# Sums of squares and means added up on VectorE and finished by one matmul, and the compressed scores of both key-value groups in one pass

## The chip, the cores and the metric

The kernel runs on one core of a Trainium2 chip. The metric is the device time of one execution in microseconds (us). TensorE (PE) does the matmuls, VectorE (DVE) and ScalarE (ACT) the elementwise work, GpSimd (POOL) a few fills, SyncE (SP) issues the transfers. Sums over partitions, which no elementwise engine does along the rows of a tile, are made by a matmul with a matrix of equal numbers as weights.

## The reference, cut to what matters

Two layers of a decoder trunk on 256 tokens of 2048 channels. The parts that the change touches are these sums:

```python
def rms_norm(x, g, eps=EPS):
    y = x32 * lax.rsqrt(jnp.mean(x32 * x32, axis=-1, keepdims=True) + eps)
...
    # conformer_conv, 512 channels
    mu = jnp.mean(h32, axis=-1, keepdims=True)
    var = jnp.mean(jnp.square(h32 - mu), axis=-1, keepdims=True)
...
    # nsa_attention: 8 query heads, 2 key-value groups, 15 compressed blocks
    s = jnp.einsum('bgrtd,bgnd->bgrtn', q, kc) * scale
    p_cmp = masked_softmax(s, cmp_mask)
    o_cmp = jnp.einsum('bgrtn,bgnd->bgrtd', p_cmp.astype(vc.dtype), vc)
...
    # hybrid_mixer: four groups of 512, each with its own norm, then one projection
    y = rms_norm(y, group_norm.reshape(N_GROUPS, GROUP_WIDTH)).reshape(B, T, MIX_WIDTH)
    return y @ w_o
...
    # each layer
    x = x + g1 * hybrid_mixer(h, ...)
    h = rms_norm(x, norm_ffn[l]) * (1.0 + sc2) + sh2
    x = x + g2 * conv_glu_ffn(h, ...)
```

## The kernel before, in words

The residual x lies transposed in SBUF: 16 chunks of 128 channels by 256 tokens. Each large product runs over weight blocks of 128 rows by 1024 columns. `load_w` (L204 to L220) has SP load a block (`raw`, four buffers), ACT round it to the fast matmul format (`hi`, L217, three buffers), and DVE take the rest (`lo` = raw − hi, L219, three buffers). `gemm_t` (L233) then does, for each of the K chunks, 24 matmuls of 256 columns on TensorE: for each of 8 output chunks hi·x, hi·xl and lo·x, x and xl being the same two parts of the activation. So every chunk needs one cast of ACT and one `lo` of DVE.

DVE also computes the modulation vectors (`ada_dot`, L159): 384 products of a 128 by 1024 block of weights with the conditioning vector, each block loaded by SP into one of three buffers `adaw`. `tick` puts them between the weight loads as filler of low priority, and the framework's scheduler settles the order of each engine's instructions when the kernel is built; the engines run their lists in that order. So a changed number of instructions in front of a place can change the order there.

A layer goes: mixing (projections, latent attention, convolution, sparse attention `nsa_group`, stick-breaking attention `sb_attn`), the output projection `wo`, the feed-forward part (11 up groups, two down projections). Four places sum over channels and are changed:

- `Stats` (L311 to L333): the sum of squares of x for the next RMSNorm, over the 16 chunks. It is called while the output chunks of the `wo` product come out (both layers), and of the last down projection of layer 0: three instances. For every two chunks ACT squares (`sq`, L320); in the first 8 chunks DVE adds the two (L324) and one fp32 matmul with ones accumulates into `ss`; in the last 8 chunks two matmuls do. `finish` takes Ln and Exp on ACT. Then `norm_chunk` makes the 16 chunks h of the feed-forward input: DVE `t` (L338), ACT `act` (L342), DVE the rest of `act` (L343), with 12 buffers `act`, so that 12 chunks are made at first.
- `group_norm_t` (L439): the norm of one group's 512 channels, used for the convolution's output and for the stick-breaking output y3, whose result is the last input of `wo`. Four fp32 matmuls (L445).
- `conv_ln` (L570): mean `mu` (L573) and variance `va` (L579) of the convolution's 512 channels, four fp32 matmuls each.
- `heads(g)` (L877): the compressed branch of group g: 8 matmuls `sc` (L890) of 15 columns, a softmax of small DVE operations, two transposes `tpx`, the product `poc`; then the two long branches of the same group.

## Time and profile before

| | us |
|---|---|
| median of 3 runs (lowest, highest) | 2482.93 (2482.63, 2484.76) |
| the profiled execution | 2479.15 |
| its span | 2476.8 |
| PE busy | 2413.6 |
| DVE busy | 1853.5 |
| ACT busy | 1165.0 |

The times within the trace count from the span's start. Outside the span lie 2479.15 − 2476.8 = 2.35 us. An fp32 matmul stands in the trace as two rows of half the work each, so "x8" of such a matmul are 4 instructions of the program; of the fast format, one row is one instruction.

### The profile page before, as it was taken

To read this page: it belongs to the slowest core of one execution; us is meant where nothing else is said; L and a number is where in the kernel's file an instruction comes from. 1 tells how busy PE (TensorE), PEld (TensorE's weight loads), DVE (VectorE), ACT (ScalarE), POOL (GpSimd) and SP (SyncE) were. 2 spreads that over 40 slices of the span, in tenths; PEclk is the share of its full clock that TensorE was granted. 3 is DMA by queue.
4 is the path that set the end of the run, shared out by engine and by line. 5 is a ranking of instruction groups with operands and counts; after the bars stand their busy time and mean duration, and the time that the engine had idled before them with its cause. 6 is when DMAs were issued, how large, how long until landed. Compare 5 with 4: busy or idle time off the path is not lost.

```text
span 2476.8 us, 46041 instructions
## 1 busy us (share of the span) xinstructions
PE 2413.6 (97%) x18720; PEld 2330.1 (94%) x18720; DVE 1853.5 (75%) x2972; ACT 1165.0 (47%) x1704; POOL 24.0 (1%) x40
## 2 busy tenths in 40 slices
PE   7888999999999999999999999999999999999999
PEld 5666999989999999999999999999999999999999
DVE  6779988898888887888767997657676676455554
ACT  2124566445545433445444576644454453344442
POOL 0000000000000000000001000000000000000000
PEclk9999999999999999999999999999999999999999
DMA  8975778988888899888875574366666666655554
GB/s 319 347 256 190 252 271 274 336 300 295 282 307 296 290 331 325 312 304 293 290 259 181 181 242 162 128 222 213 221 207 233 230 207 222 187 176 191 184 182 162
DMA packets 169125, 610.31 MB, mean 246 GB/s; under 512 B 19025, under 2 KB 20945, under 8 KB 168401
## 3 DMA queue, kind: packets, MB, share of 16 engines
q1 hardware_dynamic: 168914, 607.39, 71.1%
q8 instruction: 146, 2.39, 0.4%
q14 instruction: 65, 0.53, 0.1%
HBM read 603.12 MB, written 4.19 MB: 245 GB/s over the span
## 4 chain that ended last, share of the span: by engine, by line
PE 85%; DVE 8%; DMA 4%; ACT 2%; issue 1%; SPq 0%; DVEq 0%; ACTq 0%
PE gt L245 71%; DMA adaw<-in_ada_dram 4%; DVE acc L565 3%; PE gt L359 2%; DVE adaw L159 2%; PE pv L266 2%; PE pn L266 1%; PE s L509 1%; PE po L535 1%; PE pq L266 1%; DVE lo L219 1%; PE tp L530 1%; PE ss L326 1%; ACT hi L217 0%; PE po L981 0%
## 5 line engine op out<-in xcount | busy, mean ns | idle before, releaser
L245 PE MATMUL gt<-act,hi 128*128 128x256 f32 x7232 | 1318.4, 284 | 4.3 <-ACT act L342 4.1
L217 ACT CAST hi<-raw 128x1024 fp32r<-128x1024 f32 (+3 forms) x716 | 739.5, 1033 | 1002.3 <-PE gt L245 831.7
L219 DVE TENSOR_TENSOR lo<-raw,hi 128x1024 fp32r<-128x1024 f32 (+3 forms) x716 | 859.1, 1203 | 388.4 <-ACT hi L217 386.6
L245 PEld LDWEIGHTS gt<-act,hi 128*128 128x128 f32 x7232 | 1129.5, 192 | 7.0 <-ACT act L342 4.9
L245 PE MATMUL gt<-act,lo 128*128 128x256 f32 x3616 | 1021.7, 285 | 3.5 <-DVE lo L219 3.4
L245 PEld LDWEIGHTS gt<-act,lo 128*128 128x128 f32 x3616 | 691.9, 192 | 4.9 <-DVE lo L219 4.7
L159 DVE SCALAR_TENSOR_TENSOR adaw<-adaw,cond 128x1024 f32<-128x1024 f32 x384 | 467.0, 1221 | 126.4 <-DMA adaw<-in_ada_dram 124.3
L245 PE MATMUL gt<-g,hi 128*128 128x256 f32 x2816 | 507.1, 283 | 0.0
L245 PEld LDWEIGHTS gt<-g,hi 128*128 128x128 f32 x2816 | 438.7, 192 | 0.2
L245 PE MATMUL gt<-g,lo 128*128 128x256 f32 x1408 | 396.9, 283 | 0.1
L245 PEld LDWEIGHTS gt<-g,lo 128*128 128x128 f32 x1408 | 269.5, 192 | 0.3 <-DVE lo L219 0.3
L359 PE MATMUL gt<-actw,raw 128*128 128x256 f32 x416 | 106.1, 418 | 26.4 <-ACT actw L340 26.4
L359 PEld LDWEIGHTS gt<-actw,raw 128*128 128x128 f32 x416 | 86.5, 211 | 45.9 <-ACT actw L340 32.3
L565 DVE SCALAR_TENSOR_TENSOR acc<-ug,vec,acc 128x256 f32<-128x256 f32 x240 | 98.9, 476 | 0.0
L1096 ACT ACTIVATE u<-gt,vec 128x256 f32<-128x256 f32 x176 | 94.2, 561 | 5.9 <-PE gt L245 3.4
L1097 DVE SCALAR_TENSOR_TENSOR u<-gt,vec,u 128x255 f32<-128x255 f32 x176 | 79.9, 474 | 3.2 <-ACT u L1096 3.2
L1100 DVE SCALAR_TENSOR_TENSOR u<-gt,vec,u 128x254 f32<-128x254 f32 x176 | 79.4, 472 | 0.0
L359 PE MATMUL gt<-act,hi 128*128 128x256 f32 x416 | 77.1, 287 | 2.1 <-ACT act L342 2.1
L359 PEld LDWEIGHTS gt<-act,hi 128*128 128x128 f32 x416 | 66.1, 195 | 2.5 <-ACT act L342 2.5
L340 ACT ACTIVATE actw<-t,sh 128x256 f32<-128x256 f32 x16 | 8.1, 507 | 121.8 <-DVE sh L414 121.3
L359 PE MATMUL gt<-act,lo 128*128 128x256 f32 x208 | 59.5, 286 | 0.0
L523 ACT ACTIVATE pt<-s,mx,scl 128x128 f32<-128x128 f32 (+1 forms) x96 | 48.4, 512 | 9.7 <-DVE mx L520 9.7
(284 smaller groups left out, 1786.2 us busy)
## 6 DMA issues: line engine op xcount, KB each, us to landing
adaw<-in_ada_dram SPq DMA_DIRECT2D x384, 512.0 KB, 5.5
raw<-in_wup_dram SPq DMA_DIRECT2D x352, 512.0 KB, 4.3
raw<-in_wdn_dram SPq DMA_DIRECT2D x176, 512.0 KB, 4.3
raw<-in_wo_dram SPq DMA_DIRECT2D x64, 512.0 KB, 4.7
raw<-in_wconv_dram SPq DMA_DIRECT2D x32, 512.0 KB, 5.5
raw<-in_wsqk_dram SPq DMA_DIRECT2D x32, 512.0 KB, 4.3
raw<-in_wlq_dram SPq DMA_DIRECT2D x32, 448.0 KB, 4.7
raw<-in_wnkv_dram SPq DMA_DIRECT2D x32, 412.0 KB, 3.1
```

The lines of the kernel that those rows point to most:

```text
L159: nc.vector.scalar_tensor_tensor(w, w, 1.0, cond[:, hf * 1024:hf * 1024 + 1024], op0=ALU.mult, op1=ALU.mult, accum_out=raw[:, hf, j:j + 1],)
L217: nc.scalar.copy(hi[:, :n], raw[:, :n])
L219: nc.vector.tensor_sub(lo[:, :n], raw[:, :n], hi[:, :n].bitcast(F32))
L245: nc.tensor.matmul(ps[m // 2][:, m % 2, :], ww[:, c], x, start=(k == 0 and i == 0 and m % 2 == 0), stop=(k == K - 1 and i == len(prods) - ...
L266: nc.tensor.matmul(o, x[:, tt * P:(tt + 1) * P], ww[:, kk * N + c0:kk * N + c1], start=(k == 0 and i == 0 and first), stop=(k == K - 1 and ...
L326: nc.tensor.matmul(self.ss[:, 0, :], ones, sq[:, q, :], start=(self.n == 2 and q == 0), stop=(self.n == KD and q == 1 - join))
L359: nc.tensor.matmul(ps[m // 2][:, m % 2, :], ww[:, m * P:(m + 1) * P], xx, start=(first and i == 0 and m % 2 == 0), stop=(last and i == len ...
L523: nc.scalar.activation(pt[:, j, :n], s[:, j, :n], AF.Exp, scale=sc2[:, j:j + 1], bias=mx[:, j:j + 1], accum_out=rs[:, tt, 2 * pr + j:2 * p ...
L565: nc.vector.scalar_tensor_tensor(acc[:, c, :], ug[:, c, j:j + T], w, acc[:, c, :], op0=ALU.mult, op1=ALU.add)
L1096: nc.scalar.activation(u[:, q, :], src[:, q, :], AF.Identity, scale=w2, bias=fb[:, i:i + 1])
L1097: nc.vector.scalar_tensor_tensor(u[:, q, 1:], src[:, q, :T - 1], w1, u[:, q, 1:], op0=ALU.mult, op1=ALU.add)
L1100: nc.vector.scalar_tensor_tensor(u[:, q, 2:], src[:, q, :T - 2], w0, u[:, q, 2:], op0=ALU.mult, op1=ALU.add)
```

## The change

Everything that was summed by several matmuls is first added on DVE:

- `Stats`: JOIN goes from 8 to 12. The squares of the first 12 chunks are added into one accumulator on DVE, and one matmul takes it; the last 4 chunks keep a matmul each. 5 matmuls in place of 12 an instance, 11 adds in place of 4.
- `group_norm_t`, `conv_ln`: `fold` adds the four chunks in two DVE operations (512 and 256 columns), and one matmul takes the sum, in place of four.
- the compressed branch: `compressed()` does both groups before the heads, with 8 matmuls of 30 columns for 16 of 15, and the softmax in half as many operations of twice the width.

In all the program has 61 matmuls fewer (45 of 256 columns, 16 `sc`), DVE 2611 instructions for 2590, ACT 4 fewer, POOL 2 fewer.

```diff
@@ -65,7 +65,7 @@
 DW_LATE = 800
...
-JOIN = 8
+JOIN = 12
...
@@ -316,19 +316,25 @@
             self.sp, self.sq, self.n = sp, sq, 0
 
         def add(self, x2):
+
             sq = self.sp.tile([P, 2, T], F32, tag=self.sq, name="sq", bufs=2)
             nc.scalar.activation(sq, x2, AF.Square)
             self.n += 2
-            join = self.n <= JOIN
-            if join:
+            if self.n == 2:
+                self.acc = act_whole()[:, 0:2, :]
+                nc.vector.tensor_add(self.acc[:, 0, :], sq[:, 0, :], sq[:, 1, :])
+                return
+            if self.n <= JOIN:
                 nc.vector.tensor_add(sq[:, 0, :], sq[:, 0, :], sq[:, 1, :])
-            for q in range(1 if join else 2):
-                nc.tensor.matmul(
-                    self.ss[:, 0, :], ones, sq[:, q, :], start=(self.n == 2 and q == 0), stop=(self.n == KD and q == 1 - join)
-                )
+                nc.vector.tensor_add(self.acc[:, 0, :], self.acc[:, 0, :], sq[:, 0, :])
+                if self.n == JOIN:
+                    nc.tensor.matmul(self.ss[:, 0, :], ones, self.acc[:, 0, :], start=True, stop=False)
+                return
+            for q in range(2):
+                nc.tensor.matmul(self.ss[:, 0, :], ones, sq[:, q, :], start=False, stop=(self.n == KD and q == 1))
 
         def finish(self):
-            r = act_whole()[:, 0, :]
+            r = self.acc[:, 1, :]
             rsqrt(r, self.ss[:, 0, :], D)
             return r
 
@@ -436,13 +442,18 @@
         nc.scalar.copy(dst[:, 0, :], src)
         nc.vector.tensor_sub(dst[:, 1, :], src, dst[:, 0, :].bitcast(F32))
 
+    def fold(dst, src):
+
+        nc.vector.tensor_add(dst, src[:, 0:2, :], src[:, 2:4, :])
+        nc.vector.tensor_add(dst[:, 0, :], dst[:, 0, :], dst[:, 1, :])
+        return dst[:, 0, :]
+
     def group_norm_t(l, o, g, mp, pp, tag):
 
         sq = mp.tile([P, 4, T], F32, tag="sq4", name="sq")
         nc.scalar.activation(sq, o, AF.Square)
         ss = pp.tile([P, 2, T], F32, tag=tag, name="ss")
-        for c in range(4):
-            nc.tensor.matmul(ss[:, 0, :], ones, sq[:, c, :], start=(c == 0), stop=(c == 3))
+        nc.tensor.matmul(ss[:, 0, :], ones, fold(sq[:, 0:2, :], sq), start=True, stop=True)
         r = mp.tile([P, T], F32, tag="r", name="r", bufs=1)
         rsqrt(r, ss[:, 0, :], 512)
...
@@ -569,14 +580,12 @@
 
     def conv_ln(l, acc, mp, pp):
         mu = pp.tile([P, 2, T], F32, tag="gp", name="mu")
-        for c in range(4):
-            nc.tensor.matmul(mu[:, 0, :], mean512, acc[:, c, :], start=(c == 0), stop=(c == 3))
+        sq = mp.tile([P, 4, T], F32, tag="sq4", name="sq")
+        nc.tensor.matmul(mu[:, 0, :], mean512, fold(sq[:, 0:2, :], acc), start=True, stop=True)
         nc.vector.tensor_sub(acc, acc, mu[:, 0:1, :].to_broadcast([P, 4, T]))
-        sq = mp.tile([P, 4, T], F32, tag="sq4", name="sq")
         nc.scalar.activation(sq, acc, AF.Square)
         va = pp.tile([P, 2, T], F32, tag="gp", name="va")
-        for c in range(4):
-            nc.tensor.matmul(va[:, 0, :], mean512, sq[:, c, :], start=(c == 0), stop=(c == 3))
+        nc.tensor.matmul(va[:, 0, :], mean512, fold(sq[:, 0:2, :], sq), start=True, stop=True)
...
@@ -845,7 +854,7 @@
 
         nqT = mp.tile([P, 4, T], F32, name="nqT")
         qa = mp.tile([P, 2, 4, 2, 64], F32, tag="qa", name="qa")
-        scls = []
+        scls = mp.tile([P, 2, 2, 4], F32, name="nscl")
         for g in range(2):
             q = nq0
             if g:
@@ -855,7 +864,7 @@
                        lambda tt: [(pq[:, tt, :], 0, 256, tt == 0)])
                 nc.scalar.copy(q.rearrange("p t h d -> p t (h d)"), pq)
             sq = mp.tile([P, 2, 4, 64], F32, tag="nsq", name="nsq")
-            scl = mp.tile([P, 2, 4], F32, tag=f"nscl{g}", name="scl")
+            scl = scls[:, g]
             sumsq(scl, q, sq)
             rsqrt(scl, scl, 64, mul="lq64")
...
@@ -874,50 +882,63 @@
                 )
...
-        def heads(g):
-            scl = scls[g]
-
-            def coef(rs, br):
-                nc.vector.tensor_mul(rs, rs, gt[:, :, 4 * g:4 * g + 4, br])
-                return rs.unsqueeze(3).to_broadcast([P, 2, 4, 64])
-
-            og = on[:, :, 4 * g:4 * g + 4, :]
+        def compressed():
 
             s = pp.tile([P, 2, T], F32, tag="S", name="sc")
-            sv = s.rearrange("p a b -> p (a b)")[:, 0:128].rearrange("p (t r n) -> p t r n", t=2, r=4)
+            sv = s.rearrange("p a b -> p (a b)")[:, 0:256].rearrange("p (t r g n) -> p t r g n", t=2, r=4, g=2)
             for tt in range(2):
                 for r in range(4):
                     nc.tensor.matmul(
-                        sv[:, tt, r, 0:NCMP], nqT[:, r, tt * P:(tt + 1) * P], kc[:, g, 0:NCMP],
+                        sv[:, tt, r, :, 0:NCMP], nqT[:, r, tt * P:(tt + 1) * P], kc[:, :, 0:NCMP],
                         start=(tt == 0 and r == 0), stop=True, skip_group_check=True,
                     )
-            cs = mp.tile([P, 2, 4, NCMP], F32, tag="cs", name="cs", bufs=2)
...
             tp = pp.tile([P, 2, T], F32, tag="T", name="tpx")
-            for tt in range(2):
-                nc.tensor.transpose(tp[:, 0, tt * P:(tt + 1) * P], cpt[:, tt].rearrange("p r n -> p (r n)"), ident)
-            cT = mp.tile([P, T], F32, tag="cT", name="cT", bufs=1)
-            nc.scalar.copy(cT, tp[:, 0, :])
+            for g in range(2):
+                for tt in range(2):
+                    nc.tensor.transpose(
+                        tp[:, g, tt * P:(tt + 1) * P], cpt[:, g, tt].rearrange("p r n -> p (r n)"), ident
+                    )
+            cT = mp.tile([P, 2, T], F32, name="cT")
+            nc.scalar.copy(cT, tp)
+            return cT, rs
+
+        cT, crs = compressed()
+
+        def heads(g):
+            scl = scls[:, g]
+
+            def coef(rs, br):
+                nc.vector.tensor_mul(rs, rs, gt[:, :, 4 * g:4 * g + 4, br])
+                return rs.unsqueeze(3).to_broadcast([P, 2, 4, 64])
+
+            og = on[:, :, 4 * g:4 * g + 4, :]
+
...
-                    po[:, tt].rearrange("p r e -> p (r e)"), cT[:, tt * P:(tt + 1) * P],
+                    po[:, tt].rearrange("p r e -> p (r e)"), cT[:, g, tt * P:(tt + 1) * P],
                     vb[:, g].rearrange("p r e -> p (r e)"),
                     start=(tt == 0), stop=True, skip_group_check=True,
                 )
-            nc.vector.tensor_mul(og, po, coef(rs, 0))
+            nc.vector.tensor_mul(og, po, coef(crs[:, g], 0))
 
 
             for br in (1, 2):
```

How the order moves, at three places. First DVE at the end of the `wo` product of layer 0 and the start of its feed-forward part. `x` is the residual's update of one chunk, `lo` the weights' second part for one chunk of the feed-forward product, `adaw` the filler, `t` the first step of a chunk of h. Before:

```order
L1061 SCALAR_TENSOR_TENSOR x<-gt,mod_2_1155,x 128x256 x8
L159 SCALAR_TENSOR_TENSOR adaw,modr_3_2228<-adaw,cond 128x1024 x2
L219 TENSOR_TENSOR lo<-raw,hi 128x1024
L338 SCALAR_TENSOR_TENSOR t_4607<-x,amul,actw 128x256
L338 SCALAR_TENSOR_TENSOR t_4611<-x,amul,actw 128x256
L219 TENSOR_TENSOR lo<-raw,hi 128x1024
L343 SCALAR_TENSOR_TENSOR act<-t_4607,mod_3_2230,act 128x256
L343 SCALAR_TENSOR_TENSOR act<-t_4611,mod_3_2230,act 128x256
L338 SCALAR_TENSOR_TENSOR t_4615<-x,amul,actw 128x256
L338 SCALAR_TENSOR_TENSOR t_4619<-x,amul,actw 128x256
L159 SCALAR_TENSOR_TENSOR adaw,modr_4_2227<-adaw,cond 128x1024
```

After the change:

```order
L1082 SCALAR_TENSOR_TENSOR x<-gt,mod_2_1155,x 128x256
L328 TENSOR_TENSOR sq<-sq 128x256
L1082 SCALAR_TENSOR_TENSOR x<-gt,mod_2_1155,x 128x256
L329 TENSOR_TENSOR actw<-actw,sq 128x256
L1082 SCALAR_TENSOR_TENSOR x<-gt,mod_2_1155,x 128x256
L159 SCALAR_TENSOR_TENSOR adaw,modr_3_2257<-adaw,cond 128x1024
L219 TENSOR_TENSOR lo<-raw,hi 128x1024 x2
L159 SCALAR_TENSOR_TENSOR adaw,modr_4_2256<-adaw,cond 128x1024 x2
L344 SCALAR_TENSOR_TENSOR t_4576<-x,amul,actw 128x256
L344 SCALAR_TENSOR_TENSOR t_4580<-x,amul,actw 128x256
L159 SCALAR_TENSOR_TENSOR adaw,modr_3_2257<-adaw,cond 128x1024
L349 SCALAR_TENSOR_TENSOR act<-t_4576,mod_3_2259,act 128x256
```

Between the last `x` and the first `t` stood three instructions, one of them a `lo`; now five, two of them `lo`; and the `lo` that followed the first two `t` is now an `adaw`. The next `lo` of before stands among the following chunks of h:

```order
L338 SCALAR_TENSOR_TENSOR t_4632<-x,amul,actw 128x256
L338 SCALAR_TENSOR_TENSOR t_4636<-x,amul,actw 128x256
L219 TENSOR_TENSOR lo<-raw,hi 128x1024
L343 SCALAR_TENSOR_TENSOR act<-t_4632,mod_3_2230,act 128x256
L343 SCALAR_TENSOR_TENSOR act<-t_4636,mod_3_2230,act 128x256
```

and of the change behind all 12 of them:

```order
L344 SCALAR_TENSOR_TENSOR t_4618<-x,amul,actw 128x256
L344 SCALAR_TENSOR_TENSOR t_4622<-x,amul,actw 128x256
L159 SCALAR_TENSOR_TENSOR adaw,modr_3_2257<-adaw,cond 128x1024
L349 SCALAR_TENSOR_TENSOR act<-t_4618,mod_3_2259,act 128x256
L349 SCALAR_TENSOR_TENSOR act<-t_4622,mod_3_2259,act 128x256
L159 SCALAR_TENSOR_TENSOR adaw,modr_4_2256<-adaw,cond 128x1024 x2
L219 TENSOR_TENSOR lo<-raw,hi 128x1024
```

So the third, fourth and fifth `lo` of the product, which before came amid the 12 chunks of h, have moved: the third now stands ahead of the first `t`, the fourth behind the twelfth chunk, and between the chunks only `adaw` is left. On PE, 72 matmuls (three chunks) stand between the last matmul of `ss` and the eight hi·x with which the fourth chunk begins.

Second, DVE at the norm of y3 in layer 0 (`osb` is y3 before and after its scaling, `act` its second part for the `wo` product). Before:

```order
L159 SCALAR_TENSOR_TENSOR adaw,modr_3_2228<-adaw,cond 128x1024
L219 TENSOR_TENSOR lo<-raw,hi 128x1024
L453 SCALAR_TENSOR_TENSOR osb<-osb,vec,r 128x256 x4
L283 TENSOR_TENSOR act<-osb,act 128x2x256
L159 SCALAR_TENSOR_TENSOR adaw,modr_3_2228<-adaw,cond 128x1024
L283 TENSOR_TENSOR act<-osb,act 128x2x256
```

After the change:

```order
L447 TENSOR_TENSOR sq<-sq 128x512
L448 TENSOR_TENSOR sq<-sq 128x256
L159 SCALAR_TENSOR_TENSOR adaw,modr_4_2256<-adaw,cond 128x1024
L219 TENSOR_TENSOR lo<-raw,hi 128x1024
L464 SCALAR_TENSOR_TENSOR osb<-osb,vec,r 128x256 x4
L219 TENSOR_TENSOR lo<-raw,hi 128x1024
L283 TENSOR_TENSOR act<-osb,act 128x2x256 x2
```

The two adds come in front, and a `lo` now stands between the scaling and the second part. On PE, 17 matmuls of the `wo` product stand between the norm's matmul and the first that reads y3; before there were 93.

Third, PE where the convolution's mean stood, in the stick-breaking projection of layer 0. `mu` came in place of a wait:

```order
L778 MATMUL tp<-con,nkv 128x128
L245 MATMUL gt<-act,hi 128x256 x2
L266 MATMUL pv<-hi,act 128x256
L573 MATMUL mu<-acc,mean_77 128x256 x4
L245 MATMUL gt<-act,lo 128x256
L245 MATMUL gt<-act,hi 128x256 x2
```

After the change `mu` has left this place:

```order
L787 MATMUL tp<-con,nkv 128x128
L245 MATMUL gt<-act,hi 128x256 x2
L266 MATMUL pv<-hi,act 128x256
L245 MATMUL gt<-act,lo 128x256
L245 MATMUL gt<-act,hi 128x256 x2
L245 MATMUL gt<-act,lo 128x256
```

It stands later, as one matmul among the scores `s` of the first heads:

```order
L524 MATMUL s<-cmask,identb 128x2x128
L584 MATMUL mu<-sq,mean_77 128x256
L541 MATMUL tp<-con,pt 128x128 x2
L520 MATMUL s<-nkT,nqT 128x128 x2
```

The matmul that reads `lo` now follows directly on the ones in front of `mu`.

## Rows read from the trace of the kernel before

**Rows 1.** The page: busy time of the engines, the chain that ended last by engine, and the transfers of the filler (count, KB each, us from issue to landing).
```profile
PE 2413.6 (97%) x18720; PEld 2330.1 (94%) x18720; DVE 1853.5 (75%) x2972; ACT 1165.0 (47%) x1704; POOL 24.0 (1%) x40
...
PE 85%; DVE 8%; DMA 4%; ACT 2%; issue 1%; SPq 0%; DVEq 0%; ACTq 0%
...
adaw<-in_ada_dram SPq DMA_DIRECT2D x384, 512.0 KB, 5.5
```
**Rows 2.** The groups of instructions by line: busy us in all, mean ns of one | idle before them and what ended it. The first five are the matmuls that the change touches; L1106 is the nearest DVE operation of 512 columns on two tensors.
```profile
L326 PE MATMUL ss<-sq,ones 128*128 128x256 f32 x72 | 19.1, 386 | 0.3 <-ACT sq L320 0.3
L445 PE MATMUL ss<-sq,ones 128*128 128x256 f32 x32 | 8.2, 394 | 1.1 <-ACT sq L442 1.1
L573 PE MATMUL mu<-acc,mean 128*128 128x256 f32 x16 | 3.8, 379 | 0.0
L579 PE MATMUL va<-sq,mean 128*128 128x256 f32 x16 | 4.4, 380 | 0.0
L890 PE MATMUL sc<-kc,nqT 128*128 128x15 f32 x64 | 7.4, 257 | 0.0
...
L324 DVE TENSOR_TENSOR sq<-sq 128x256 f32<-128x256 f32 x12 | 5.1, 423 | 0.0
L1106 DVE TENSOR_TENSOR u<-u,sg 128x512 f32<-128x512 f32 x44 | 30.0, 682 | 0.0
```
**Rows 3.** The chain of waits in order of time (start us, us, what): pieces of the chain that are such matmuls.
```profile
311.74 1.69 PE sc L890 x16
...
437.19 1.97 PE ss L445 x8
...
1284.61 3.73 PE ss L326 x16
...
1705.83 1.73 PE ss L326 x8
```
**Rows 4.** Timelines of DVE, ACT and PE at the end of layer 1's `wo` product (start us, us, engine, line, operation): the last eight updates of x, the first step of h, the Ln of `finish`, and the last matmuls of `ss`.
```profile
1703.71 3.22 DVE L1061 SCALAR_TENSOR_TENSOR x<-gt,mod,x 128x256 f32<-128x256 f32 x8 [1.42 <-PE gt L245]
1710.54 0.88 DVE L338 SCALAR_TENSOR_TENSOR t<-x,amul,actw 128x256 f32<-128x256 f32 x2 [1.34 <-ACT actw L288]
...
1709.59 0.47 ACT L286 ACTIVATE actw<-ss,scal 128x256 f32<-128x256 f32 x1 [1.32 <-PE ss L326]
...
1705.67 3.88 PE L326 MATMUL ss<-sq,ones 128*128 128x256 f32 x16
```
**Rows 5.** Timeline of DVE at the start of layer 0's feed-forward part: the last updates of x, then `lo`, `t`, filler and `lo` in turn.
```profile
507.50 3.23 DVE L1061 SCALAR_TENSOR_TENSOR x<-gt,mod,x 128x256 f32<-128x256 f32 x8 [0.18 <-PE gt L245]
...
512.93 1.22 DVE L219 TENSOR_TENSOR lo<-raw,hi 128x1024 fp32r<-128x1024 f32 x1
514.84 0.88 DVE L338 SCALAR_TENSOR_TENSOR t<-x,amul,actw 128x256 f32<-128x256 f32 x2 [0.69 <-ACT actw L288]
515.64 1.22 DVE L219 TENSOR_TENSOR lo<-raw,hi 128x1024 fp32r<-128x1024 f32 x1
...
517.57 0.87 DVE L338 SCALAR_TENSOR_TENSOR t<-x,amul,actw 128x256 f32<-128x256 f32 x2
...
523.85 1.22 DVE L219 TENSOR_TENSOR lo<-raw,hi 128x1024 fp32r<-128x1024 f32 x1
...
526.72 1.22 DVE L219 TENSOR_TENSOR lo<-raw,hi 128x1024 fp32r<-128x1024 f32 x1
...
534.03 1.22 DVE L219 TENSOR_TENSOR lo<-raw,hi 128x1024 fp32r<-128x1024 f32 x1
```
**Rows 6.** Timeline of PE in the same stretch: the last matmuls of `ss`, the first of the feed-forward product, and the wait at its sixth chunk.
```profile
512.72 1.13 PE L326 MATMUL ss<-sq,ones 128*128 128x256 f32 x4 [0.34 <-ACT sq L320]
515.92 1.22 PE L245 MATMUL gt<-act,hi 128*128 128x256 f32 x4 [2.07 <-ACT act L342]
...
532.20 1.12 PE L245 MATMUL gt<-act,hi 128*128 128x256 f32 x8
535.30 0.39 PE L245 MATMUL gt<-act,lo 128*128 128x256 f32 x1 [1.98 <-DVE lo L219]
```
**Rows 7.** Busy time by stretch (from:to, us; then PE, PEld, DVE, ACT and POOL busy with their counts, the granted clock, the DMA share, GB/s).
```profile
536.40:539.80 3.40, 3.40 (x18) 3.40 (x18) 3.09 (x4) 1.04 (x1) 0.00 (x0) 0.50 0.93 348
...
220.00:440.00 220.00, 216.45 (x1648) 202.52 (x1647) 196.53 (x379) 143.63 (x313) 5.69 (x9) 0.99 0.76 259
...
275.00:330.00 55.00, 54.01 (x447) 51.08 (x447) 51.85 (x111) 33.00 (x74) 0.31 (x1) 1.00 0.69 240
```
**Rows 8.** Timelines of DVE and ACT at the norm of y3 in layer 0: the scaling, the second part for the `wo` product, and the Ln of the norm.
```profile
440.16 1.67 DVE L453 SCALAR_TENSOR_TENSOR osb<-osb,vec,r 128x256 f32<-128x256 f32 x4 [0.48 <-ACT r L288]
441.75 0.68 DVE L283 TENSOR_TENSOR act<-osb,act 128x512 fp32r<-128x512 f32 x1
...
439.20 0.47 ACT L286 ACTIVATE r<-ss,scal 128x256 f32<-128x256 f32 x1 [1.16 <-PE ss L445]
```
**Rows 9.** Timelines of PE and DVE around the convolution's mean in layer 0.
```profile
287.53 1.89 PE L573 MATMUL mu<-acc,mean 128*128 128x256 f32 x8
290.17 0.38 PE L245 MATMUL gt<-act,lo 128*128 128x256 f32 x1 [0.75 <-DVE lo L219]
...
288.90 1.22 DVE L219 TENSOR_TENSOR lo<-raw,hi 128x1024 fp32r<-128x1024 f32 x1
```
**Rows 10.** Timeline of PE in the first heads of layer 0, where `va` and `poc` stand between scores and transposes.
```profile
315.33 1.03 PE L579 MATMUL va<-sq,mean 128*128 128x256 f32 x4
...
317.61 1.13 PE L915 MATMUL poc<-vb,cT 128*128 128x256 f32 x4
```

More of the change, by code (lines that the diff above doesn't have):

```diff
@@ L866, in nsa_group @@
             nc.vector.tensor_add(qa[:, :, :, g, :], q, u)
-            scls.append(scl)
         for r in range(4):
@@ L876, in nsa_group @@
                 nc.scalar.copy(nqT[:, r - 1:r + 1, :], tp)
+        def compressed():
+            s = pp.tile([P, 2, T], F32, tag="S", name="sc")
+            sv = s.rearrange("p a b -> p (a b)")[:, 0:256].rearrange("p (t r g n) -> p t r g n", t=2, r=4, g=2)
+            for tt in range(2):
+                for r in range(4):
+                    nc.tensor.matmul(
+                        sv[:, tt, r, :, 0:NCMP], nqT[:, r, tt * P:(tt + 1) * P], kc[:, :, 0:NCMP],
+                        start=(tt == 0 and r == 0), stop=True, skip_group_check=True,
+                    )
+            cs = mp.tile([P, 2, 8, NCMP], F32, name="cs")
+            cs8 = cs.rearrange("p t (r g) n -> p (t r) g n", g=2)
+            nc.vector.tensor_mul(
+                cs8, sv.rearrange("p t r g n -> p (t r) g n")[:, :, :, 0:NCMP],
+                scls.rearrange("p g t r -> p (t r) g").unsqueeze(3).to_broadcast([P, 8, 2, NCMP]),
+            )
+            nc.vector.tensor_add(cs, cs, xm.unsqueeze(2).to_broadcast([P, 2, 8, NCMP]))
+            mx = mp.tile([P, 2, 8], F32, name="cmx")
+            nc.vector.tensor_reduce(mx, cs, axis=AX.X, op=ALU.max)
+            nc.vector.tensor_scalar_max(mx, mx, 0.1 * NEG)
+            nc.vector.tensor_sub(cs, cs, mx.unsqueeze(3).to_broadcast([P, 2, 8, NCMP]))
+            cpt = mp.tile([P, 2, 2, 4, 32], F32, name="cpt")
+            nc.gpsimd.memset(cpt, 0.0)
+            nc.scalar.activation(cpt.rearrange("p g t r n -> p (t r) g n")[:, :, :, 0:NCMP], cs8, AF.Exp)
+            rs = mp.tile([P, 2, 2, 4], F32, name="crs")
+            nc.vector.tensor_reduce(rs, cpt, axis=AX.X, op=ALU.add)
+            nc.vector.tensor_scalar_max(rs, rs, 1e-30)
+            nc.vector.reciprocal(rs, rs)
+            tp = pp.tile([P, 2, T], F32, tag="T", name="tpx")
+            for g in range(2):
+                for tt in range(2):
+                    nc.tensor.transpose(
+                        tp[:, g, tt * P:(tt + 1) * P], cpt[:, g, tt].rearrange("p r n -> p (r n)"), ident
+                    )
+            cT = mp.tile([P, 2, T], F32, name="cT")
+            nc.scalar.copy(cT, tp)
+            return cT, rs
+        cT, crs = compressed()
         def heads(g):
-            scl = scls[g]
+            scl = scls[:, g]
             def coef(rs, br):
```

20 lines of the change are left out of this document (removed).

## The prediction

> **What bounds the kernel now.** I read the page first: PE is busy 97% of the span and DVE 75%, and the chain that ended last is 85% PE, 8% DVE, 4% transfers [rows 1]. So a matmul taken away is a gain as a rule, and an added DVE operation is free as a rule. I next read the groups by line for the counts and means [rows 2], and the chain for prices: there the pitch counts, since a matmul's mean in a pipelined queue contains its wait behind the one before [rows 3]. Last I read timelines and stretches where the change alters the order of instructions. There the rule of the page is weakest: over 220 to 440 us DVE is busy 196.53 of 220, that is 89%, and over 275 to 330 us 51.85 of 55, 94% [rows 7]; and at the start of layer 0's feed-forward part PE waits for DVE, 1.98 us in one row [rows 6].
>
> The sum is made against the profiled execution, 2479.15 us (span 2476.8 and 2.35 around it). The median of the runs lies 2482.93 − 2479.15 = 3.8 above it, which I add at the end.
>
> **What goes from PE.** In the chain, 4 fp32 matmuls of 256 columns (eight rows) take 1.73 us [rows 3], so one costs 0.43 us. Eight `sc` of 15 columns (16 rows) take 1.69, that is 0.21 each.
>
> - `Stats`, first half: 4 matmuls in three instances are gone, 12 × 0.43 = 5.2. Against it, in the two `wo` products DVE now does more adds between the eight x updates that release the PSUM banks; with an add at 0.42 [rows 2] and some two more ahead of the last release, 0.75 each, 1.5 in all. Net +3.7.
> - `Stats`, second half: the stretch from the first of the last eight x updates to Ln is 1709.59 − 1703.71 = 5.88 [rows 4]. PE has 8 matmuls there now, 5 after. But 4 adds come between the updates of x. Eight updates take 3.15 (3.22 less the overlap at the end) or 0.395 each; with four adds at 0.35 (0.42 less the same overlap) the last x ends at 4.6, then come ACT's square 0.63, two matmuls 0.87 and passing on 0.3: 6.4. Loss 0.55 in two instances, −1.1; layer 0's `wo` is counted below.
> - `group_norm_t`: 4 instances, 3 matmuls each, 12 × 0.43 = +5.2. The adds (0.68 for 512 columns [rows 2], 0.42 for 256) lie beside the products on PE, except at y3 of layer 0, below.
> - `va`: 6 × 0.43 = +2.6.
> - `mu`: nothing gained where it stood. PE went from its four matmuls into a wait of 0.75 for a `lo` that started at 288.90 and reached PE at 290.17, and the DVE rows in front of that `lo` are the same in the order [rows 9]. Without `mu` PE waits there 2.64 in place of 0.75. The one matmul left stands later, in busy PE: −0.43 in each layer, −0.9. Were the `lo` earlier by what DVE is late from other causes, up to 1.7 a layer would be won: bound +3.4.
> - `sc`: 16 × 0.21 = +3.4, if 30 columns cost what 15 do. At 0.106 us a row PE does a row in the time that 256 columns of the fast format take (0.12: eight in 1.12 with the drain of the last [rows 6]), so the columns are not the price; the weight load is.
>
> Sum of this list: 3.7 − 1.1 + 5.2 + 2.6 − 0.9 + 3.4 = +12.9.
>
> **What it costs: three places.**
>
> *First heads of layer 0 and 1.* `va` and `poc` stand between the scores and the transposes that wait for DVE and ACT [rows 10]: cover. Where the softmax behind sets the time, taking `va` away wins nothing. That is between nothing and the 1.3 us of `va` a layer with some 0.2 of the moved transposes, 3.0 in both. I take half, −1.5: neither row shows a wait ahead of it, but with less cover one may come.
>
> *y3 of layer 0.* Before, 93 matmuls of `wo` stood between the norm and its first reader; now 17, 17 × 0.12 = 2.0 us. From Ln at 439.20 the scaling ends at 440.16 + 1.67 = 441.83, 2.63 later [rows 8]; the order now puts a `lo` of 1.14 and two second parts of 0.68 (the first counts) behind: 2.63 + 1.14 + 0.68 = 4.45. PE is ready 2.0 after its matmul: a stall of 2.4 if the norm's matmul comes as PE reaches it, and 3.3 where the filler and `lo` that stand between the adds and the scaling (2 × 1.15) come first. −2.8; bounds 0 (if PE is late anyway) and −4.
>
> *Start of layer 0's feed-forward part.* Before, the first x of the last eight is at 507.50, the first `t` at 514.84, 7.34 later, and Ln is not the limit by much (the wait was 0.69) [rows 5]. In the order after, the last x ends at 4.6 (above), then A, L, L, A, A (filler A or `lo` L, 1.15 each: the 1.22 of the `lo` rows less the overlap with the next): 4.6 + 5 × 1.15 = 10.35. So `t` is 3.0 later. From there each two chunks of h take 2.73 with one filler or `lo` among them (514.84 to 517.57 [rows 5]). Before, three `lo` came in these slots, at 515.64, 523.85, 526.72; the next, chunk 6's, began at 534.03, and PE waited for it at 535.30, 20.5 after the first `t` [rows 5, 6]. After, the slots hold filler alone: the `lo` of chunk 4 comes behind six pairs, two fillers and itself, 6 × 2.73 + 3 × 1.15 + 0.6 for passing on, also some 20.4 after the first `t`. At that time PE starts on the `lo` of chunk 4 where before it started on that of chunk 6: two chunks of 24 × 0.12 = 2.9 each, 5.8, are still to do. With the 3.0: −9.0, a little more where a filler waits for its transfer (5.5 us from issue to landing [rows 1], three buffers): −9.1. PE would stand still about 8 us there in one piece. After 1.98 the granted clock was 0.50 for a stretch of 3.4 us (18 matmuls, 0.19 each in place of 0.12 [rows 7]); the start before has that fall already, so I add nothing for it.
>
> The term depends on PE not going on to later work. The row shows that it doesn't: it did the eight hi·x that stand in front in its order, then nothing for 1.98 [rows 6]. The Trainium skill (TensorE: Matmul & The Clock Gate, section "The mechanism" of Part 3) says that matmuls start and end in program order and that only weight loads are drawn ahead; by it, and by the row, the term stands. Could PE pass the blocked chunk, the term would be 3.0 in place of 9.1, and the time 6 lower, 2477.
>
> **Sum.** 12.9 − 1.5 − 2.8 − 9.1 = −0.5: 2479.15 + 0.5 = 2479.65 on the profiled execution's scale, 2479.65 + 3.8 = 2483.5. I say 2483.
>
> **Rivals.**
>
> *A. Faster: PE is the bound and the start of the feed-forward part costs no more than before.* For it: 97%, and the gains lie in stretches where PE waits for nothing. Against it: the order, in which the three `lo` have left. If the filler passes faster or the product's fourth chunk is not late, 12.9 − 1.5 is left: 2483 − 11 = 2472. The profile would show PE's wait at the start of the feed-forward part as small as before.
>
> *B. Slower: in layer 0's mixing DVE is the bound.* DVE takes 512 + 256 column adds there and longer compressed operations in a stretch with 89% (94% in its middle) busy [rows 7]; it decides where DVE exceeds some 95%, as PE's work then waits for `lo`. Then layer 0's share of the savings (`va` 1.3, group norm 2.6, `sc` 1.7, together 5.6) turns into waits, and fillers that came close behind one another wait for their transfers, about 1.2 at the start of the feed-forward part: −0.5 − 5.6 − 1.2 = −7.3, 2490.
>
> *C. The saved matmuls were hidden anyway.* Against it: they stand in the chain [rows 3], for instance 3.73 us at 1284.61. Only `mu` is hidden, already in the sum. Without any gain, the costs alone (−13.4) would give 2496; the chain speaks so plainly against it that it gets 0.03, out of B's share.
>
> **How the numbers follow.** My forecast 0.44, rival A 0.32, B with C 0.24. The unknowns of the forecast itself are: heads ±1.5, y3 −1.2 to +2.8, `mu` up to +3.4, the start ±1.5: its own range is 2478 to 2488. The range over the cases, with A's end near 2471 and B's near 2490.5: 2471 to 2491. No change means within 0.2%, 5 us, which is about what a measurement of this kernel can tell. From the forecast 0.38 of its 0.44 falls inside, 0.04 faster, 0.02 slower; of A a fifth (0.06) stays inside; of B a quarter (0.05): faster 0.30, same 0.49, slower 0.21.
>
> **What would show it.** Right: in the profile after, PE waits about 8 us for `lo` after the third chunk of layer 0's feed-forward product, with a first `t` some 10 us behind the first of the last eight x; at 288 to 290 the same `lo` ends PE's wait, now 2.6 long; PE's matmul groups of `ss`, `mu`, `va`, `sc` shrink from 19.1 + 8.2 + 3.8 + 4.4 + 7.4 to under half; the layer 1 stretches are shorter by about 5 us. Wrong: a start of the feed-forward part with waits as before (then A), or many new waits for `lo` between 220 and 440 (then B).

## The result, and the profile after

The changed kernel takes 2507.89 us (median of 6 runs, 2492.58 to 2510.73), the kernel before 2482.94 (2480.18 to 2486.82): a ratio of 1.0085, 95% interval 1.0066 to 1.0103, so 16 to 26 us slower. The forecast was 2483, the range 2471 to 2491. The profiled execution took 2508.80, 29.65 more than that of before. By the medians the loss is 25 us, by the ratio, which goes by the means, 21.

The page of the kernel after: engines, chain, and mean granted clock by core.

```profile
PE 2408.0 (96%) x18598; PEld 2322.9 (93%) x18598; DVE 1867.1 (74%) x2993; ACT 1164.0 (46%) x1700; POOL 24.3 (1%) x38
...
PE 77%; DVE 11%; DMA 7%; ACT 3%; issue 2%; SPq 0%; DVEq 0%; ACTq 0%
...
core 0: 2506.6 us, clock 0.986
```

The matmuls are gone: 122 rows fewer than in [rows 1], and these groups answer to [rows 2]:

```profile
L334 PE MATMUL ss<-sq,ones 128*128 128x256 f32 x24 | 7.8, 473 | 0.0
...
L891 PE MATMUL sc<-kc,nqT 128*128 128x30 f32 x32 | 3.9, 264 | 0.0
...
L331 PE MATMUL ss<-actw,ones 128*128 128x256 f32 x6 | 2.6, 516 | 6.8 <-DVE actw L329 6.8
L456 PE MATMUL ss<-sq,ones 128*128 128x256 f32 x8 | 2.6, 401 | 0.9 <-DVE sq L448 0.9
```

`sc` went from 7.4 to 3.9 us for half as many matmuls: one of 30 columns cost what one of 15 did. But the three matmuls of L331 were preceded by 6.8 us of waiting, and PE's share of the chain fell from 85% to 77%, while that of DVE rose from 8% to 11% and that of transfers from 4% to 7%. The clock's mean fell from 0.992 in the execution of before to 0.986.

Both kernels issue the same 16272 matmuls of the large products (`gt`), in the same order of chunks, so the start of the n-th of them tells where the time went. The table gives the difference to the first trace of before, by stretch (times of before), with a second trace of either kernel, taken later. The column "implied" is what the prediction's sum implied (minus is a gain).

```
stretch (us)                                implied  change  change, 2nd  before, 2nd
0-262     up to the stick-breaking product     0.0     +5.0       +1.0         +3.1
262-437   its product, sparse heads           -3.1     +2.9       +0.6         -1.4
437-462   norm of y3                          +1.5     +7.8       +6.3          0.0
462-507   rest of wo, layer 0                 -1.0     -1.6       -1.6          0.0
507-545   start of feed-forward, layer 0      +9.1    +13.6      +12.9         +3.3
545-1221  feed-forward, layer 0                0.0     +3.3      +10.3         +3.8
1221-1283 last down projection                -1.7     -1.3       -1.3          0.0
1283-1469 start of layer 1                    +0.5     +0.5       +0.4         -1.4
1469-1665 heads, y3 and wo, layer 1           -5.4     -2.4       -1.2         -0.5
1665-1729 start of feed-forward, layer 1      +0.5     +2.1       +3.5          0.0
after                                          0.0      0.0        0.0          0.0
sum                                           +0.5    +29.9      +30.9         +6.9
```

The second trace of the unchanged kernel is 6.9 us longer than the first, by three stretches (before 262, 507 to 545, 545 to 1221); so some 7 of the change's 30 us may be scatter.

Two rows have to be read together. Before, the last matmuls of the stick-breaking attention (`z`, `po`) end ahead of 437. In the changed kernel's order 20 rows of them, some 3.0 us of PE's time, stand behind the `gt` matmul that ends the second row (it starts at 444.9 in the trace after), among the products in front of the norm of y3. The same is seen in all runs that have both fold and the compressed pass, in the one without the part in `conv_ln` with 10 rows. The first and the last of these rows, and the norm's matmul:

```profile
446.08 0.70 PE L997 MATMUL z<-ssp,con 128*128 128x256 f32 x2
...
453.23 0.39 PE L1003 MATMUL po<-sa,sv 128*128 128x128 f32 x2
...
458.82 0.67 PE L456 MATMUL ss<-sq,ones 128*128 128x256 f32 x2 [0.90 <-DVE sq L448]
```

So the row 262-437 shows some 3.0 too little loss and the row 437-462 as much too much: with that moved back they are +5.9 and +4.8, in the second trace +3.7 and +3.2.

The rest of the loss is at a few places. PE's waits from 220 to 620 us, in the kernel after (engine, line, what was waited for: us in all, times, longest):

```profile
PE gt L245 <- DVE lo L219: 11.0, 4, 7.5
PE tp L541 <- ACT pt L534: 5.2, 4, 2.0
...
PE ss L331 <- DVE actw L329: 3.3, 1, 3.3
...
PE gt L245 <- ACT act L282: 1.5, 1, 1.5
...
PE ss L456 <- DVE sq L448: 0.9, 1, 0.9
PE gt L245 <- DVE act L283: 0.6, 1, 0.6
```

Before, `lo` stood at 2.7; none of the other waits shown was there. The wait for the first h of the feed-forward part (`act`, L342) was 2.1 and is 2.3 after the change:

```profile
PE gt L245 <- DVE lo L219: 2.7, 2, 2.0
PE gt L245 <- ACT act L342: 2.1, 1, 2.1
```

The four waits for `pt`, the softmax of the long branches, are two in the first heads and two in the second:

```profile
323.55 0.77 PE L541 MATMUL tp<-con,pt 128*128 128x128 f32 x2 [1.31 <-ACT pt L534]
...
326.29 0.98 PE L541 MATMUL tp<-con,pt 128*128 128x128 f32 x4 [0.84 <-ACT pt L534]
...
379.10 0.48 PE L541 MATMUL tp<-con,pt 128*128 128x128 f32 x1 [2.05 <-ACT pt L534]
...
393.74 0.77 PE L541 MATMUL tp<-con,pt 128*128 128x128 f32 x2 [1.02 <-ACT pt L534]
```

The start of layer 0's feed-forward part, after (timelines of DVE and PE), answers to [rows 5, 6]:

```profile
522.59 1.66 DVE L1082 SCALAR_TENSOR_TENSOR x<-gt,mod,x 128x256 f32<-128x256 f32 x4
...
532.91 0.88 DVE L344 SCALAR_TENSOR_TENSOR t<-x,amul,actw 128x256 f32<-128x256 f32 x2
...
552.84 1.22 DVE L219 TENSOR_TENSOR lo<-raw,hi 128x1024 fp32r<-128x1024 f32 x1
...
554.12 0.58 PE L245 MATMUL gt<-act,lo 128*128 128x256 f32 x1 [7.55 <-DVE lo L219]
```

From the first x to the first `t` are 10.32 us, and PE stands still for 7.55 at the fourth chunk. What comes behind that wait is seen in the stretches (columns as in [rows 7]): three stretches of 3.4 us at or near half clock, where before one came behind the wait of 1.98.

```profile
554.10:557.50 3.40, 3.38 (x16) 3.38 (x17) 2.33 (x5) 0.00 (x0) 0.00 (x0) 0.50 0.91 294
557.50:560.90 3.40, 2.80 (x13) 2.51 (x13) 3.40 (x10) 1.95 (x3) 0.00 (x0) 0.50 0.90 337
560.90:564.30 3.40, 3.40 (x21) 3.40 (x21) 2.76 (x6) 0.54 (x1) 0.00 (x0) 0.63 0.86 313
```

### The profile page after: what moved, and what is told of

Same layout as the page of the kernel before. It is cut to its first block, busy times and chain, and to the rows that moved or that the text cites. A ratio compares the mean times of both kernels' runs of the same rounds, so it can differ in the third digit from the quotient of the medians.

```text
span 2506.6 us, 45808 instructions
## 1 busy us (share of the span) xinstructions
PE 2408.0 (96%) x18598; PEld 2322.9 (93%) x18598; DVE 1867.1 (74%) x2993; ACT 1164.0 (46%) x1700; POOL 24.3 (1%) x38
## 4 chain that ended last, share of the span: by engine, by line
PE 77%; DVE 11%; DMA 7%; ACT 3%; issue 2%; SPq 0%; DVEq 0%; ACTq 0%
PE gt L245 65%; DMA adaw<-in_ada_dram 6%; DVE acc L576 2%; DVE adaw L159 2%; DVE lo L219 2%; PE gt L365 2%; PE pn L266 1%; PE pv L266 1%; PE po L546 1%; PE pq L266 1%; PE s L520 1%; PE tp L541 1%; ACT hi L217 1%; ACT pt L534 0%; DVE x L1139 0%
## 5 line engine op out<-in xcount | busy, mean ns | idle before, releaser
L266 PE MATMUL pv<-hi,act 128*128 128x256 f32 x256 | 48.1, 285 | 0.0
```

The lines of the kernel that those rows point to most:

```text
L266: nc.tensor.matmul(o, x[:, tt * P:(tt + 1) * P], ww[:, kk * N + c0:kk * N + c1], start=(k == 0 and i == 0 and first), stop=(k == K - 1 and ...
```

## The experiments

Theory O: the saved matmuls do gain, and the loss comes from what the shortened sums move: at a few places a `lo`, a norm or a softmax is now what PE waits for. Rival W: the added DVE operations cost by themselves, wherever they stand. Each ratio is against the kernel before in runs on the same chip.

**Stats alone.** The edit is the part of the diff in `Stats` with JOIN at 12.

> Only the change of Stats, the rest as before. Theory O (the order that the schedule falls into at a few places costs the time, the saved matmuls gain): here the third to fifth lo stand among the 12 chunks of h again, so the start of layer 0's feed-forward part loses about 1 us and the rest gains 5.2 - 1.5 - 1.1: about 2481. Rival W (the adds on DVE themselves cost the time wherever they stand): slower than before by 5 or more, 2488 or above.

2494.89 us, ratio 1.0032 (1.0015 to 1.0048): W's figure came, O's 2481 did not. The start of the feed-forward part was 2.7 longer over 507 to 545, for some 1 by the order; but the profiled execution lost 20 us in 545 to 1221, where little but the places of fillers differs. It was the slowest of the ten, 2505.58, so a good part of those 20 us is its own. The longest piece there:

```profile
932.93 0.58 PE L245 MATMUL gt<-g,lo 128*128 128x256 f32 x1 [6.05 <-DVE lo L219]
```

That `lo` stood on DVE behind a filler that waited 5.83 us for its transfer and eight updates of x. Whether W or chance did it, this run couldn't tell.

**fold alone.** The parts of the diff in `group_norm_t` and `conv_ln`.

> Only fold: group norms, mean and variance; the rest as before. Theory O: 77 matmuls stand between the norm of y3 and its first reader, and the start of the feed-forward part is as before: gain 5.2 + 2.6 - 0.9, less at most 1.3 a layer of cover: 2475 to 2479. Rival W: 2485 or above. Rival V (the waits of the first heads for the softmax come from the missing va matmuls): waits of PE for pt of 3 us or more at 311 to 330 here.

2495.45 us, 1.0035 (1.0021 to 1.0049). O's figure missed by 16 and W's came, though the start of the feed-forward part and the cover of y3 were as O said. V's waits came in smaller pieces: at 311 to 330 PE waits 1.1 us for `pt` and 0.5 for `cT`, where V had named 3 or more (timeline of PE):

```profile
320.43 0.71 PE L514 MATMUL s<-nkT,nqT 128*128 128x128 f32 x4 [0.44 <-ACT pt L528]
...
322.11 1.13 PE L918 MATMUL poc<-vb,cT 128*128 128x256 f32 x4 [0.46 <-ACT cT L915]
...
325.81 0.77 PE L535 MATMUL tp<-con,pt 128*128 128x128 f32 x2 [0.69 <-ACT pt L528]
...
1606.15 1.22 PE L979 MATMUL z<-ssp,con 128*128 128x256 f32 x2 [3.48 <-DVE ssp L978]
```

The last is new too: in layer 1 the stick-breaking attention waits for DVE, where before the four matmuls of the convolution's norm had stood close ahead of its first `z`. The whole change does not have this wait: in neither of its traces does PE wait for `ssp` in layer 1.

**The compressed pass alone.** The part of the diff from `scls` to `heads`.

> Only the compressed pass; the rest as before. Theory H (the pass in front takes sc, tpx and their time from the heads, where they covered the first softmax): PE waits for pt by 3 us or more in the first heads of each layer, against 3.4 gained; with the start of the feed-forward part, where the fifth lo comes behind the 12 chunks, 2484 to 2490. Rival V (the waits come from the missing va matmuls): no such waits here, 2480.

2493.34 us, 1.0028 (1.0012 to 1.0044). In the first heads, at 311 to 330, there was no wait for `pt`; they came with the second heads (1.48 at 369.81, 0.46 at 375.23, 0.66 at 382.98). So the pass takes cover too, but from the later heads, and in layer 0 alone: layer 1 has no wait for `pt`. Neither theory's time came, 2480 by V or at most 2490 by H; in the trace 507 to 545 is 6.6 us longer and 545 to 1221 9.1. V holds for the first heads and H, in kind, for the second.

**The whole change, with `lo` early.** One priority raised:

```diff
-        nc.vector.tensor_sub(lo[:, :n], raw[:, :n], hi[:, :n].bitcast(F32))
+        early[0] -= 1
+        with tc.high_priority(offset=300) if 0 <= early[0] else ExitStack():
+            nc.vector.tensor_sub(lo[:, :n], raw[:, :n], hi[:, :n].bitcast(F32))
```

> The whole change, with a higher priority for the first six lo of layer 0's feed-forward part, so that three of them stand among the 12 chunks again; nothing else is edited. Theory O: PE's wait of 7.8 us for the fourth chunk falls under 2 and the stretch at half clock behind it goes: 9 to 11 us less than the change, 2497 to 2500 by the profiled runs. Rival W: within 3 us of the change.

2497.24 us, 1.0045 (1.0020 to 1.0069), against 1.0085, 10 us less by the ratios where W allowed 3. The time came as O said, but the wait did not go, so the figure was partly luck: over 507 to 545 the loss fell by 6.0, from 13.6 to 7.6, and in the trace another 6.2 fell in 262 to 437, which the edit was not meant to touch. The wait moved to two places: 4.46 us ahead of the accumulator's matmul, since two `lo` now stand among the last updates of x, and 4.54 at a later chunk.

```profile
518.66 1.19 PE L335 MATMUL ss<-actw,ones 128*128 128x256 f32 x2 [4.46 <-DVE actw L333]
...
550.03 0.39 PE L249 MATMUL gt<-act,lo 128*128 128x256 f32 x1 [4.54 <-DVE lo L223]
```

**The kernel before, again**, unchanged, for a second trace.

> The kernel before, unchanged, for a second trace. Theory N (the waits for fillers in layer 0's feed-forward part, 2 to 17 us in the traces of the parts, come and go from run to run): PE waits for lo in 620 to 1280 us here too, 2 to 8 us, and the same program's times spread by 10 us or more. Rival E (they come from the edits): no such waits here, as in the first trace, and times within 3 us.

2483.68 us, 0.9998 (0.9982 to 1.0015), from 2477.49 to 2491.25; PE waited for `lo` once in 620 to 1280, 2.4 us. Theory N holds in kind: that stretch scatters. A second trace of the whole change lost 10.3 there, its first 3.3.

**The whole change without the part in `conv_ln`** (mean and variance keep four matmuls each).

> The whole change without the part in conv_ln: mean and variance keep four matmuls each. Theory V (the va and mu matmuls covered the softmax of the first heads, and what the schedule makes of their absence sets the start of the feed-forward part and the norm of y3): five lo stand ahead of the fourth pair of h, 47 matmuls behind the norm of y3; PE's waits for pt at 311 to 330 fall by half or more; 10 to 17 us less than the whole change, 2491 to 2498. Rival S (the compressed pass alone costs most): 2500 or above.

2491.47 us, 1.0026 (1.0008 to 1.0044). The waits for `pt` in 262 to 480 fell from 5.2 to 2.1 us and none is left at 311 to 330; at y3 one wait of 1.32 is left, for the two adds, and the stall behind it is gone. The time is the one forecast, and V and the cover of y3 are borne out.

**Stats with JOIN at 8.**

> Stats alone with JOIN at 8: the first 8 chunks go into one accumulator and one matmul, the last 8 as before, so no add is in the last stretch; the order at the start of the feed-forward part is nearly that of before. Theory O: 9 matmuls gone, 3.9 gained, 1.5 lost at the banks: 2 to 3 us less than before on the same chip. Rival W (adds between the updates of x cost by themselves): 3 us or more above before.

2490.50 us, 1.0023 (1.0008 to 1.0037): slower, as W said, but the trace shows a reason that is neither theory's. In layer 0's last down projection PE stood still for the accumulator:

```profile
1236.92 1.22 PE L331 MATMUL ss<-actw,ones 128*128 128x256 f32 x2 [6.15 <-DVE actw L329]
```

Its matmul stands at the end of the first half's product in PE's list; the two last adds stand on DVE behind two `lo`:

```profile
1233.84 1.22 DVE L219 TENSOR_TENSOR lo<-raw,hi 128x1024 fp32r<-128x1024 f32 x1
1234.97 0.42 DVE L328 TENSOR_TENSOR sq<-sq 128x256 f32<-128x256 f32 x1
1235.31 1.22 DVE L219 TENSOR_TENSOR lo<-raw,hi 128x1024 fp32r<-128x1024 f32 x1
1236.44 0.42 DVE L329 TENSOR_TENSOR actw<-actw,sq 128x256 f32<-128x256 f32 x1
```

**Group norm folded, JOIN at 8.**

> Group norm folded and Stats with JOIN at 8; mean, variance and compressed branch as before. Theory O: 21 matmuls gone, 9.1 gained less 1.5, and 50 matmuls cover the norm of y3: 5 to 8 us less than before on the same chip. Rival W: 3 us or more above before. Rival Z (the matmuls of the conv output's norm covered the stick-breaking waits for ssp): PE waits for ssp of 3 us or more in a layer, and no gain.

2496.17 us, 1.0041 (1.0027 to 1.0055): O's 5 to 8 us less did not come, W's and Z's figures did. The same block of 6 us, and Z's wait for `ssp` in layer 1 as with fold, again 3.48 us: the mean and the variance, which stand as before here, are not its cause. It stands in the three kernels that fold the group norm and leave the compressed branch as before (fold alone, this one, and the change without the compressed pass) and in none that has the compressed pass.

**The whole change, again.**

> The whole change, unchanged, for a second trace and for times beside the parts. If the waits found in its first trace (fourth chunk of layer 0's feed-forward product 7.8 us, pt in the first heads 3.6 and 5, y3 some 4) are the program's and not that execution's, they stand here within 1 us each; 16 to 26 us above before.

2509.85 us, 1.0087 (1.0060 to 1.0115). The fourth chunk waited 7.5, `pt` 4.0 in all for 5.2, y3 2.5 for 3.0: the waits stand at the same places, all but one within 1 us, and so are the program's.

**JOIN at 8 with the matmul late.**

```diff
-                if self.n == JOIN:
-                    nc.tensor.matmul(self.ss[:, 0, :], ones, self.acc[:, 0, :], start=True, stop=False)
                 return
+            if self.n == JOIN + 2:
+                nc.tensor.matmul(self.ss[:, 0, :], ones, self.acc[:, 0, :], start=True, stop=False)
```

> As Stats alone with JOIN at 8, but the accumulator's matmul is issued with the fifth pair of chunks and no longer with the fourth. Theory P (its place in PE's list, ahead of the second half's product while the last two adds stand behind lo on DVE, made the wait of 6.2 us in layer 0's last down projection): that wait is gone and the time is 6 to 9 us less than with the early matmul, within 3 us of before. Rival W (the adds cost by themselves): 5 us or more above before.

2480.89 us, 0.9991 (0.9979 to 1.0003): some 8 us less than with the early matmul by the two ratios, and the wait is gone. Both kernels have the same adds, so W is out for these.

**The change without the compressed pass**, and **without Stats**:

> The change without the compressed pass. Theory O (order): three lo stand among the 12 chunks of h, 77 matmuls behind the norm of y3, so neither the long wait at the start of the feed-forward part nor the stall at y3 comes, only fold's waits in the heads and the later tails: 2490 to 2497. Additive theory (each part costs what it cost alone, 9.8 and 10.3): 2501 to 2506.

> The change without Stats. Theory O: waits for pt in the heads of both kinds (those of fold and those of the compressed pass, some 8 us a layer with the clock), 17 matmuls behind the norm of y3 and its stall of 3 to 8 us, and three lo ahead of the fifth pair of h (the fourth chunk waits some 4 us): 2497 to 2505, and the stall at y3 stands here although Stats is as before. If y3's stall is absent: the theory of its cover is wrong.

2492.78 us, 1.0026 (1.0014 to 1.0039), and 2496.03 us, 1.0050 (1.0030 to 1.0070), the second 1 us under its forecast. The parts don't add: by the medians Stats and fold cost 9.8 and 10.3 alone and 8.5 together, as O had said: with both, the `lo` stand among the chunks of h again, and 507 to 545 is 1.7 longer, not 13. Adds that cost by themselves, wherever they stand, would have added up to some 20; so W is not what made the two losses, though a small cost of each add is not excluded. Without Stats, the stall at y3 stands as in the whole change, 1.49 for the adds, 1.54 and 0.60 behind:

```profile
453.76 0.67 PE L450 MATMUL ss<-sq,ones 128*128 128x256 f32 x2 [1.49 <-DVE sq L442]
...
457.99 0.74 PE L245 MATMUL gt<-act,hi 128*128 128x256 f32 x4 [1.54 <-ACT act L282]
459.33 0.39 PE L245 MATMUL gt<-act,hi 128*128 128x256 f32 x1 [0.60 <-DVE act L283]
```

**Three more runs**: the late matmul again, the same with `lo` early, and the whole change with JOIN at 8 and the late matmul.

> Stats with JOIN at 8 and the late matmul, again, for a narrower interval: 9 matmuls gone and no new wait, 3.9 gained less what the adds cost at the banks and 0.43 in each tail: 1 to 4 us less than before. If the first figure was chance: within 1 us of before or above it.

> The same with the higher priority for the first six lo of layer 0's feed-forward part: the sixth lo stands at the fifth pair of h, so PE's wait of 2.0 us there and the half clock behind it go; one lo among the updates of x delays the first t by some 0.7: 2 to 4 us less than without it, 2477 to 2481. If the lo order matters only where the change had moved it: no difference.

> The whole change with JOIN at 8 and the late matmul. Theory O: at the start of layer 0's feed-forward part two lo stand ahead of t and two among the 12 chunks, PE's wait of 7.8 becomes 2 to 3, and no tail waits for an accumulator: 10 to 14 us less than the whole change; the waits in the heads (4 to 5 us for pt) and at y3 stay: 2495 to 2500. Rival: the start of the feed-forward part isn't where the time is: above 2503.

2479.95 us, 0.9989 (0.9975 to 1.0004); 2482.44, 0.9990 (0.9977 to 1.0004); 2496.95, 1.0054 (1.0033 to 1.0074). The late matmul alone came out 3.4 and 4.4 us under before by the medians of its two series (2.2 and 2.7 by the ratios), each interval just reaching 1, so a gain is not shown; it is what 3.9 us of matmuls, less little, would give. The early `lo` added nothing to it: the forecast of 2 to 4 us less missed. In the last kernel the stretch 507 to 545 fell from +13.6 and +12.9 to +3.4, the wait for `lo` in it from 7.5 to 2.0, with the waits at y3 as in the change and those for `pt` no smaller (6.7). So the start of the feed-forward part and the tails are 12 to 13 us of the change's 25 by the medians, 8 of its 21 by the ratios; the trace, of an execution 10 us over its median, gives 11 to 13 for 507 to 545 and layer 1's tail.

## Why the prediction was wrong

The sum of gains less costs was to be −0.5; it was about −25 by the medians, −21 by the ratio. Two things failed: the price of lost cover in the heads, which the sum put at 1.5 us, and the clock behind new waits, which it put at nothing. By its steps:

- **What goes from PE**: the prices held where nothing waits. The `wo` product of layer 0 gained 1.6 for a forecast 1.0, the last down projection 1.3 for 1.7, `sc` halved. `mu` won nothing where it stood, as said: the wait there became 2.48 us (2.64 forecast).

```profile
295.52 0.39 PE L245 MATMUL gt<-act,lo 128*128 128x256 f32 x1 [2.48 <-DVE lo L219]
```

- **Start of layer 0's feed-forward part**: mechanism and place right. First `t` after 10.32 us (10.35 forecast), wait 7.55 (about 8), but the term of 9.1 came out as 13.6 and 12.9; the second trace of before lost 3.3 of that without any change. Missing was the clock: "I add nothing for it". Before, one stretch stood at 0.50 behind the wait for the first h and one behind that for `lo`. After, the first fall went on through a second stretch, at 0.67, and the other through three, 0.50, 0.50 and 0.63; 3.4 us times 0.33 + 0.50 + 0.37 is some 4 us, about what the first trace lost beyond the term. The accumulator's matmul made PE wait as well (3.3 us, L331), but the first `t` came no later for it. The Trainium skill (TensorE: Matmul & The Clock Gate, section "Why this matters for your kernels") asks to avoid idle gaps in the middle of a kernel because the clock is lowered after them; this trace agrees, 0.50 after the wait of 7.55. The first fall, before and after:

```profile
515.90:519.30 3.40, 3.21 (x13) 2.92 (x14) 3.40 (x6) 1.28 (x3) 0.00 (x0) 0.50 0.94 377
```

```profile
533.90:537.30 3.40, 3.14 (x13) 2.85 (x14) 2.96 (x7) 1.34 (x4) 0.00 (x0) 0.50 0.90 277
537.30:540.70 3.40, 3.40 (x22) 3.40 (x22) 3.40 (x7) 0.92 (x1) 0.00 (x0) 0.67 0.79 251
```

- **y3 of layer 0**: the waits were right, the clock was missing again. The waits were 0.90 + 1.54 + 0.60 = 3.0, forecast 2.8. With the moved matmuls of the stick-breaking attention taken off, the stretch lost 4.8 and 3.2 where 1.5 was implied. The difference between the two traces is the clock behind the stall: 0.71 and 0.78 in two stretches of the first, which is 1.7 us, and 1.00 in the second. What is left, some 2 us, is not traced.

```profile
463.00:466.40 3.40, 2.74 (x13) 2.54 (x14) 3.40 (x6) 0.53 (x2) 0.00 (x0) 0.71 0.99 366
466.40:469.80 3.40, 3.40 (x25) 3.40 (x24) 2.22 (x5) 1.05 (x1) 0.00 (x0) 0.78 1.06 433
```

- **First heads**: this is the step that failed most. It allowed 1.5 us in both layers, at most 3.0, since "neither row shows a wait ahead of it". A row without a wait only says that the cover was enough. In the change PE waits 5.2 us for `pt` in layer 0 alone, 4.0 in the second trace, and 1.9 in layer 1 in both. The two parts of the change each take a piece of the cover (fold in the first heads, the compressed pass in the second), so in layer 0 the gains of `va`, `sc` and the convolution's folded norm (1.3 + 1.7 + 1.3 us) became waits: with the moved matmuls put back, that stretch lost 5.9 and 3.7 where a gain of 3.1 was implied, 9.0 and 6.8 short. In layer 1 a gain of 2.4 and 1.2 is left of 5.4. That is what rival B had for layer 0, by another mechanism: not DVE's share, which was 87% over 220 to 440 for 89% before and at most 94% in a piece of 30 us, so that B's condition, some 95%, was not met, but a chain over DVE and ACT that PE's other work no longer covered. With the four matmuls each of mean and variance back, the waits at 311 to 330 were gone. Behind the two later waits the clock fell too, to 0.50 after 2.05 us and to 0.56 after 1.02, which is another 3.2 us.
- **The later tails**: +0.55 forecast, in layer 1 it was 2.1 and 3.5. The x to `t` stretch did lengthen by 0.65 (7.5 from 1731.4 to 1738.89, 6.83 in [rows 4]), and the clock fell here too: 0.67 and 0.83 in the first two stretches of the feed-forward product, 1.00 and 1.00 before, which is 1.7 us. What is new ahead of them is a wait of 1.82 for the accumulator's matmul (L331); the wait for the first h is 2.07 in both kernels.

```profile
1739.90:1743.30 3.40, 3.33 (x19) 3.33 (x20) 3.17 (x8) 1.33 (x4) 0.00 (x0) 0.67 0.88 284
1743.30:1746.70 3.40, 3.40 (x26) 3.40 (x26) 1.28 (x2) 1.86 (x3) 0.00 (x0) 0.83 0.46 186
```

- **The chances**: the range ended where rival B did, and no case had two of the costs at once. They did come together. What they share, as I read the traces: sums that PE made between its products kept it busy while another chain ran, and sums on DVE stand in DVE's list behind whatever the schedule puts there. Rival A's time was too low as well: it dropped the stall at y3 with the start of the feed-forward part, which it doesn't depend on; with the 2.8 it is 2475 and not 2472.

What stays open: how much of the change's loss in 545 to 1221 (3.3 and 10.3 against 0 and 3.8) is the program's; but for a few matmuls within one chunk, only the places of fillers differ there.

## What to carry to other kernels

A matmul taken from a busy TensorE gains its time only where what comes behind it is ready: before pricing it, ask how long the chain behind would have waited without it, because a trace without waits doesn't say how much cover is left. Where a sum moves to an engine that also feeds TensorE, read the new order at every place that TensorE waits for that engine, and issue the matmul that takes the sum later than the work that can run without it: with Stats alone that was worth some 8 us here. Add to a new wait the slower clock that may follow it: here it lasted three stretches after the wait of 7.55 and followed some of the shorter waits, not all.
